# Dilated attention by token classes, an earlier turn of the fourth tile, and a projection started beside a rotation

## The chip, the cores and the metric

One of the eight cores of a Trainium2 chip runs the kernel; the metric is the time of one execution on the device in microseconds (us). The engines are TensorE (PE, with its weight loads as PEld), VectorE (DVE), ScalarE (ACT), GpSimd (POOL) and SyncE (SP), which only issues DMAs here.

## What is computed

Two transformer blocks on 512 tokens of width 1024, one after the other, in 32-bit floats. The first block is an FFN, a hybrid mixer and a second FFN; the mixer adds a branch of latent attention over the 128 best keys of an indexer and a branch of dilated attention, each under a gate. The second block is a mixer of MLA and retention, whose two halves are joined and projected, and a layer of experts found by keys (PEER). The part of the reference that is rewritten is the dilated branch: three groups of four heads, each with a window and a dilation, and a softmax over the groups by their log sums.

```python
DIL_PAIRS = ((128, 1), (512, 4), (2048, 16))

def dilated_group(q, k, v, window, dilation):
    offs = jnp.arange(window // dilation + 1) * dilation
    ...
        idx = tq[:, None] - offs[None, :]
        valid = idx >= 0
    ...
        s = jnp.where(valid[None, :, None, :], s, -jnp.inf)
        lse = jax.nn.logsumexp(s, axis=-1)
        p = jnp.exp(s - lse[..., None])
    ...
    wts = jax.nn.softmax(jnp.stack(lses, axis=0), axis=0)
    o = jnp.sum(wts[..., None].astype(v.dtype) * jnp.stack(outs, axis=0), axis=0)
```

A token of the second group sees the earlier tokens of its own class modulo 4, one of the third group those of its own class modulo 16, which lie in the same class modulo 4.

## The kernel before

Tokens are handled in four tiles of 128 (`NT` is 4, `P` is 128). A large product of 32-bit numbers is three products of split halves (`mm3`, lines 126 to 128): `h_hi` and `h_lo` for the activations, `whi` and `wlo` for the weights. Weights come by SP's queue (`raw`) and are split by ACT and DVE (`split`). PSUM tiles come from three rings, `ps`, `sc` and `po`. The instructions of each engine run in the order of its queue; that order is that of the code, in which generators yield so that two stages take turns, smoothed by a scheduler that sees the whole program.

At a boundary between sublayers (`boundary`) each tile's last products are joined to the residual `x`, its mean square is taken, the tile is scaled into `xs`, transposed on PE (`turn`, L414) and split into `h_hi` and `h_lo`. The first two tiles are turned inside the boundary; the third and fourth are handed on as two calls, `late[0]` (which also scales the fourth tile) and `late[1]`. The next sublayer calls them between its first products: `ffn` in its first chunk, where three products of 1024 by 128 are done in two halves of 256 tokens; `nform_steps` (latents of the first mixer and of MLA) between token tiles t = 0 to 3; `peer_queries` between its four blocks.

Dilated attention (`dilated`) treats two pairs of heads per group, pair after pair. For a pair, three parts (q, k, v) of width 384 are projected for all tiles; q and k are rotated (`rope`, six DVE operations, L606 to L611, into `dr`) and transposed by head pair (L885) into `dqT` and `dkT`; v stays as `dv`. Twelve chains follow, three groups for each of four query tiles, in a pipeline of three stages: first the scores (L623), masks added by a product with the identity (L628, one for each 128 keys), maximum, exponential; second the transposes of the exponentials (L642); third the products with v (L648). All groups see all key blocks up to their own (the first group two at most), so masked scores are computed too. After the third group of a tile `dil_join` weighs the three outputs. Between the rounds stand steps of the gate products (six products of width 512 each), and `merge` lets the indexer of the other branch run beside it: scores L786, then sixteen rounds of maximum and replacement on DVE (L799, L800) for each of three tiles. `heads_attend` of the latent branch follows.

In the second block `mixer2` runs MLA to the end (`oa`), then the retention in two halves: `ret_queries(1)` projects q and k of the second half, and only when all its tiles are done does it rotate and transpose them one by one (`then`, L611 to L1242); `ret_mix(0)` stands between its products. Then `oa` is transposed into `mT`, and the first eight steps of the output projection (`project_start`, six products each) fill the gaps of `ret_mix(1)`. A last fact for reading: L139 and L137 are the copies out of PSUM (`evac`), which alternate between ACT and DVE.

## Time and profile before

| | |
|---|---|
| time of the runs, us | 2829.49 median of 3 (2829.47 to 2831.88) |
| profiled execution, its own time | 2831.28 us |
| its span, first to last instruction | 2829.3 us |
| mean granted clock of PE | 0.989 |
| PE busy | 2757.3 us, 97% |
| DVE busy | 2058.4 us, 73% |
| ACT busy | 1151.5 us, 41% |
| POOL busy | 368.9 us, 13% |

A matmul's end is modelled and the next one starts before it, so the price of one is read from start to start where it can be. In a wait, the engine named behind the arrow is the one whose result was waited for last. PEclk 1.00 is the 2.4 GHz level, 0.50 the 1.2 GHz level.

### The profile page before, as it was taken

How to read it: one execution, taken by the hardware profiler on the slowest of the kernel's cores; microseconds unless marked ns; L12 is line 12 of the kernel's file. 1: busy time of each engine (PE TensorE's matmuls, PEld its weight loads, DVE VectorE, ACT ScalarE, POOL GpSimd, SP SyncE). 2: the span in 40 equal slices, each digit the busy share in tenths (PEclk: the TensorE clock that was granted, in tenths of full speed). 3: DMA queues.
4: the chain of work that ended last, by engine and by line, in shares of the span. 5: the costliest groups of instructions: out<-in, count | busy, mean ns of one | idle time of the engine just before them, and what ended most of it. 6: DMA issues, size and time to landing. Idle time of an engine off the chain costs nothing. (4 is left out here: it accounts for less than half of the span.)

```text
span 2829.3 us, 38970 instructions
## 1 busy us (share of the span) xinstructions
PE 2757.3 (97%) x14629; PEld 2331.7 (82%) x14629; DVE 2058.4 (73%) x4396; ACT 1151.5 (41%) x1925; POOL 368.9 (13%) x367
## 2 busy tenths in 40 slices
PE   8999999999999999999998999999999999999998
PEld 5877787879788777887787888999988888989896
DVE  6895247895656787226756789999877778877887
ACT  4343244333535444225523433765633333333333
POOL 0000000000000000001001002111121115343451
PEclk9999999999999999999999999999999999999999
DMA  7664221212034564321121227888899999888894
GB/s 276 223 235 144 89 103 47 93 61 90 16 132 147 190 228 178 112 99 63 61 67 74 90 96 246 310 290 299 318 347 330 328 322 336 326 313 307 300 344 181
DMA packets 152524, 552.55 MB, mean 195 GB/s; under 512 B 12368, under 2 KB 61840, under 8 KB 112656
## 3 DMA queue, kind: packets, MB, share of 16 engines
q1 hardware_dynamic: 111040, 403.86, 39.3%
q0 software_dynamic: 38848, 140.56, 14.0%
q10 hardware_dynamic: 2448, 5.65, 0.5%
q8 instruction: 114, 1.87, 0.3%
q14 instruction: 74, 0.61, 0.1%
HBM read 505.56 MB, written 44.47 MB: 194 GB/s over the span
## 5 line engine op out<-in xcount | busy, mean ns | idle before, releaser
L120 ACT ACTIVATE whi<-raw 128x1024 fp32r<-128x1024 f32 (+2 forms) x489 | 508.0, 1040 | 799.0 <-PE ps L127 381.6
L121 DVE TENSOR_TENSOR wlo<-raw,whi 128x1024 fp32r<-128x1024 f32 (+2 forms) x489 | 585.9, 1199 | 299.7 <-ACT whi L120 296.1
L126 PE MATMUL ps<-h_hi,whi 128*128 128x384 f32 (+2 forms) x1912 | 693.6, 363 | 10.8 <-ACT h_hi L131 6.4
L128 PE MATMUL ps<-h_hi,wlo 128*128 128x384 f32 (+2 forms) x1912 | 685.4, 359 | 3.1 <-DVE wlo L121 3.1
L127 PE MATMUL ps<-h_lo,whi 128*128 128x384 f32 (+2 forms) x1912 | 687.0, 359 | 0.7 <-DVE h_lo L132 0.7
L126 PEld LDWEIGHTS ps<-h_hi,whi 128*128 128x128 f32 x1912 | 362.1, 190 | 47.3 <-ACT h_hi L131 6.9
L128 PEld LDWEIGHTS ps<-h_hi,wlo 128*128 128x128 f32 x1912 | 361.9, 189 | 34.9 <-DVE wlo L121 4.0
L127 PEld LDWEIGHTS ps<-h_lo,whi 128*128 128x128 f32 x1912 | 362.6, 190 | 31.4 <-DVE h_lo L132 1.1
L126 PE MATMUL acc<-whi,wh 128*128 128x512 f32 x768 | 303.7, 396 | 2.4 <-ACT wh L131 2.4
L128 PE MATMUL acc<-whi,wl 128*128 128x512 f32 x768 | 303.9, 396 | 0.2 <-DVE wl L132 0.2
L127 PE MATMUL acc<-wlo,wh 128*128 128x512 f32 x768 | 303.7, 396 | 0.0
L1552 POOL DMA_INDIRECT erow<-in_eu,ids x128 | 142.5, 1113 | 651.1 <-DVE junk L1556 477.7
L131 ACT ACTIVATE wh<-wv 128x384 fp32r<-128x384 f32 x128 | 67.1, 524 | 339.7 <-issue 165.9
L1552 POOL DMA_INDIRECT erow<-in_ev,ids x128 | 166.7, 1302 | 225.6 <-DVE eacc L1564 194.1
L128 PEld LDWEIGHTS acc<-whi,wl 128*128 128x128 f32 x768 | 144.4, 188 | 35.9 <-DVE wl L132 0.8
L126 PEld LDWEIGHTS acc<-whi,wh 128*128 128x128 f32 x768 | 144.3, 188 | 35.9 <-ACT wh L131 2.7
L127 PEld LDWEIGHTS acc<-wlo,wh 128*128 128x128 f32 x768 | 144.4, 188 | 32.9
L1564 DVE SCALAR_TENSOR_TENSOR eacc<-erow,wgt,eacc 128x1024 f32<-128x1024 f32 x127 | 162.8, 1282 | 5.1 <-DMA erow<-in_ev,ids 3.5
L285 DVE SCALAR_TENSOR_TENSOR rows<-mraw,sil,rows 128x256 f32<-128x256 f32 x336 | 160.3, 482 | 6.6
L132 DVE TENSOR_TENSOR wl<-wv,wh 128x384 fp32r<-128x384 f32 x128 | 71.3, 557 | 122.5 <-ACT wh L131 114.8
L1556 DVE SCALAR_TENSOR_TENSOR junk<-erow,xr 128x1024 bf16<-128x1024 f32 x128 | 155.4, 1219 | 4.9 <-DMA erow<-in_eu,ids 4.9
L126 PE MATMUL ps<-whi,h_hi 128*128 128x384 f32 (+3 forms) x400 | 145.9, 366 | 7.1 <-ACT h_hi L131 6.5
(507 smaller groups left out, 4377.5 us busy)
## 6 DMA issues: line engine op xcount, KB each, us to landing
raw<-in_euT SPq DMA_DIRECT2D x64, 1024.0 KB
raw<-in_evp SPq DMA_DIRECT2D x64, 1024.0 KB
raw<-in_gu SPq DMA_DIRECT2D x44, 1024.0 KB
mraw<-in_wmod SPq DMA_DIRECT2D x24, 1024.0 KB
mraw<-in_wada SPq DMA_DIRECT2D x24, 1024.0 KB
dg<-gb SPq DMA_DIRECT2D x24, 1024.0 KB
gt<-dg SPq DMA_DIRECT2D x16, 1536.0 KB
raw<-in_dn SPq DMA_DIRECT2D x22, 1024.0 KB
```

The lines of the kernel that those rows point to most:

```text
L120: self.nc.scalar.activation(hi, r, AF.Copy)
L121: self.last_low = self.nc.vector.tensor_tensor(lo, r, hi.bitcast(F32), op=OP.subtract)
L126: mm(out, l[0], r[0], start=start, stop=False)
L127: mm(out, l[0], r[1], start=False, stop=False)
L128: self.last_mm = mm(out, l[1], r[0], start=False, stop=stop)
L131: self.nc.scalar.activation(hi, v, AF.Copy)
L132: self.last_pair = self.nc.vector.tensor_tensor(lo, v, hi.bitcast(F32), op=OP.subtract)
L285: nc.vector.scalar_tensor_tensor(rows, rv[:, k, :], c, rows, op0=OP.mult, op1=OP.add)
L1552: nc.gpsimd.indirect_dma_start(out=row, out_offset=None, in_=src, in_offset=bass.IndirectOffsetOnAxis(ap=ids[:, m:m + 1], axis=0))
L1556: nc.vector.scalar_tensor_tensor(junk, row, 1.0, xr, op0=OP.mult, op1=OP.mult, accum_out=act[:, m:m + 1])
L1564: nc.vector.scalar_tensor_tensor(eacc, row, wg[:, m:m + 1], eacc, op0=OP.mult, op1=OP.add)
```

## The change

Four things are edited. (1) Dilated attention: the first group keeps its chains over tiles of consecutive tokens, four per pair; the second and third group are computed together by classes modulo 4, four chains per pair: 128 queries against the 128 keys of their own class, one causal mask and one causal mask of every fourth, side by side in 256 columns. To this end q and k of these two groups are written into `dqT` and `dkT` in class order; v is projected first, written to DRAM (`dvs`) and read back twice, in token order (`dv`) and in class order (`cv`); the first group's outputs, maxima and sums go to DRAM (`dgs`) and come back in class order (`g0`), read after round `NT + 1` of the pipeline, for `dil_join`, which now runs per class; the transposed result `bT` is written back in token order. All of these DMAs are on POOL's queue, 11 per pair. The masks come first in their accumulation, and are a product of 256 columns. (2) The fourth tile is turned one block of products earlier in the FFN, the two latents and PEER's queries. (3) In `mixer2` the transposes of `oa` and four of the eight steps of `project_start` move into `ret_queries(1)`, the steps between its rotations; `mT` becomes two tiles, one for each half of the inner dimension. (4) Weights are packed in the order v, q, k.

```diff
-    m = [causal, k >= q, causal & ((q - k) % 4 == 0), (q - k) % 4 == 0,
-         causal & ((q - k) % 16 == 0), (q - k) % 16 == 0]
+    m = [k >= q, causal, causal & ((q - k) % 4 == 0)]
...
-                            if not j:
-                                late_h[n]()
+                            if not n and j in (0, 2):
+                                late_h[j // 2]()
...
-                    if late and t in (0, 3):
-                        late[t // 3]()
+                    if late and t in (0, 2):
+                        late[t // 2]()
...
             then(t, out[t][:, :width])
+            yield
...
+        self.dvs = [dg.tile([S, 384], F32, name=f"dvs{n}") for n in range(2)]
+        self.dgs = [dg.tile([S, 132], F32, name=f"dgs{n}") for n in range(2)]
...
-            dv = dil.tile([P, NT, 384], F32, name="dv")
+            dv = dil.tile([P, NT, P], F32, name="dv")
+            cv = dil.tile([P, NT, 256], F32, name="cv")
+            g0 = dil.tile([P, NT, 132], F32, name="dg0")
...
-                    if part == 2:
-                        self.evac(dv[:, t, :], out[t][:, :384])
+                    if part == 0:
+                        vt = self.misc.tile([P, 384], F32, name="dvt", tag="v")
+                        self.evac(vt, out[t][:, :384])
+                        nc.gpsimd.dma_start(self.dvs[pr][ts], vt)
...
-                    self.evac(dT[part][:, :, ts], p[:, :384].rearrange("p (g e) -> p g e", e=P))
+                    z = dT[part - 1]
+                    self.evac(z[:, 0, ts], p[:, :P])
+                    self.evac(z[:, 1:].rearrange("p g (j c) -> p g j c", j=NT)[:, :, :, 32 * t:32 * t + 32],
+                              p[:, P:384].rearrange("p (g m j) -> p g j m", g=2, j=NT))
+                if part == 0:
+                    nc.gpsimd.dma_start(dv, self.dvs[pr][:, :P].rearrange("(t p) e -> p t e", p=P))
+                    nc.gpsimd.dma_start(cv, self.dvs[pr][:, P:].rearrange("(c j) e -> c j e", j=NT))
...
+            mk = self.masks.rearrange("p a k -> p (a k)")
             for i in range(NT):
-                st = {}
-                for g in range(3):
-                    b0 = max(0, i - 1) if g == 0 else 0
-                    nb = i + 1 - b0
-                    masks = [(b * P, m[:, 2 * g + (0 if b == nb - 1 else 1), :]) for b in range(nb)]
-                    segs = []
-                    for s in range(2):
-                        rows = slice(64 * s, 64 * s + 64)
-                        segs.append((dT[0][rows, g, i * P:(i + 1) * P], dT[1][rows, g, b0 * P:(i + 1) * P], masks,
-                                     [dv[:, b0 + b, g * P + s * 64:g * P + s * 64 + 64] for b in range(nb)]))
-                    chains.append(self.dil_chain(work, st, segs, g, ob[:, i, pr * P:(pr + 1) * P]))
+                b0 = max(0, i - 1)
+                qs, ks = slice(i * P, (i + 1) * P), slice(b0 * P, (i + 1) * P)
+                heads = [([(dT[0][r, 0, qs], dT[1][r, 0, ks])],
+                          [[dv[:, b, 64 * s:64 * s + 64] for b in range(b0, i + 1)]])
+                         for s, r in enumerate((slice(0, 64), slice(64, P)))]
+                chains.append(self.dil_chain(work, heads, mk[:, (b0 - i + 1) * P:2 * P], self.dgs[pr][qs], None, None))
+            for j in range(NT):
+                js = slice(j * P, (j + 1) * P)
+                heads = [([(dT[0][r, g, js], dT[1][r, g, js]) for g in (1, 2)],
+                          [[cv[:, j, (g - 1) * P + 64 * s:(g - 1) * P + 64 * s + 64]] for g in (1, 2)])
+                         for s, r in enumerate((slice(0, 64), slice(64, P)))]
+                chains.append(self.dil_chain(work, heads, mk[:, P:], None, g0[:, j], ob[:, j, pr * P:(pr + 1) * P]))
...
+                if n == NT + 1:
+                    nc.gpsimd.dma_start(g0, self.dgs[pr].rearrange("(c j) e -> c j e", j=NT))
...
+    def dil_chain(self, work, heads, mask, dram, g0, out):
+        nc = self.nc
+        nb, w = len(heads[0][0]), mask.shape[-1]
+        st = {}
         def first():
-            if g == 0:
-                st["po"] = self.ps("po")
+            p = [self.ps(), self.ps()]
+            for s in range(2):
+                nc.tensor.matmul(p[s][:, :w], self.idb, mask, start=True, stop=False)
+            for b in range(nb):
+                for s in range(2):
+                    q, k = heads[s][0][b]
+                    nc.tensor.matmul(p[s][:, b * P:b * P + k.shape[-1]], q, k, start=False, stop=b == nb - 1)
+            if dram is not None:
+                st["z"] = work.tile([P, 132], F32, name="dz", tag="dz", bufs=4)
+                st["neg"], st["sums"] = st["z"][:, 128:130], st["z"][:, 130:132]
+            else:
                 st["neg"] = self.small.tile([P, 8], F32, name="neg", tag="neg")
                 st["sums"] = self.small.tile([P, 8], F32, name="sums", tag="sums")
-            for s, seg in enumerate(segs):
-                n = 2 * g + s
-                fs.append(self.attend(work, seg, 0.125, st["po"][:, n * 64:(n + 1) * 64], st["neg"], st["sums"], n))
-            for i in range(2):
-                for f in fs:
-                    f[i]()
+            lead = 0 if nb == 1 else 2
+            st["pr"] = []
+            for s in range(2):
+                mx = self.small.tile([P, 2], F32, name="mx", tag="mx")
+                nc.vector.tensor_reduce(mx[:, :nb], p[s][:, :w].rearrange("p (b k) -> p b k", b=nb), axis=AX.X, op=OP.max)
+                ng = st["neg"][:, lead:lead + 2 * nb].rearrange("p (b s) -> p s b", s=2)[:, s]
+                nc.vector.tensor_scalar(ng, mx[:, :nb], -0.125, None, op0=OP.mult)
+                pr = work.tile([P, 256], F32, name="pr", tag="pr", bufs=4)
+                for b in range(nb):
+                    n = lead + 2 * b + s
+                    bs = slice(b * (w // nb), (b + 1) * (w // nb))
+                    nc.scalar.activation(pr[:, bs], p[s][:, bs], AF.Exp, bias=st["neg"][:, n:n + 1], scale=0.125,
+                                         accum_out=st["sums"][:, n:n + 1])
+                st["pr"].append(pr)
         def second():
-            for f in fs:
-                f[2]()
+            st["pT"] = []
+            for pr in st["pr"]:
+                pt = self.ps("sc")
+                for b in range(w // P):
+                    nc.tensor.transpose(pt[:, b * P:(b + 1) * P], pr[:, b * P:(b + 1) * P], self.idf)
+                pT = work.tile([P, 256], F32, name="pT", tag="pT", bufs=4)
+                self.evac(pT[:, :w], pt[:, :w])
+                st["pT"].append(pT)
         def third():
-            for f in fs:
-                f[3]()
-            if g == 2:
-                self.dil_join(work, st["po"], st["neg"], st["sums"], out)
+            po = self.ps("po")
+            for s in range(2):
+                n = 0
+                for b, vals in enumerate(heads[s][1]):
+                    o = po[:, (2 * b + s) * 64:(2 * b + s + 1) * 64]
+                    for i, v in enumerate(vals):
+                        nc.tensor.matmul(o, st["pT"][s][:, n * P:(n + 1) * P], v, start=i == 0, stop=i == len(vals) - 1)
+                        n += 1
+            if dram is not None:
+                self.evac(st["z"][:, :P], po[:, :P])
+                nc.gpsimd.dma_start(dram, st["z"])
+            else:
+                self.dil_join(work, po, g0, st["neg"], st["sums"], out)
...
+        nc.gpsimd.tensor_copy(neg[:, :2], g0[:, 128:130])
+        nc.gpsimd.tensor_copy(sums[:, :2], g0[:, 130:132])
...
-                    self.transposed(ob[:, t, :], 2, t, bT[0], bT[1])
+                    self.transposed(ob[:, t, :], 2, 0, *(z.rearrange("p k (c j) -> p k j c", j=NT)[:, :, t] for z in bT))
...
+                pool = self.pool(st, "turneda", side="right", reuse_waits="tile")
+                aT = [pool.tile([P, 4, S], F32R, name=n) for n in ("aTh", "aTl")]
+                mT = [[z] for z in aT]
                 mix = self.ret_mix(0, t0, oy)
+                y = [[] for _ in range(NT)]
+                start = self.project_start(a["wo2"], mT, y)
                 for n, _ in enumerate(self.ret_queries(1, t1, h)):
-                    if n % 2:
-                        next(mix, None)
+                    if n < 16:
+                        if n % 2:
+                            next(mix, None)
+                        if n % 4 == 3:
+                            self.transposed(oa[:, n // 4, :], 4, n // 4, *aT, tag="sc")
+                    else:
+                        next(start)
                 for _ in mix:
                     pass
             pool = self.pool(st, "turned2", side="right", reuse_waits="tile")
-            mT = [pool.tile([P, KD, S], F32R, name=n) for n in ("mTh", "mTl")]
+            rT = [pool.tile([P, 4, S], F32R, name=n) for n in ("rTh", "rTl")]
...
-            if n % 2 == 0:
-                late[n // 2]()
+            if n < 2:
+                late[n]()
...
-        for part in range(3):
+        for part in (2, 0, 1):
```

On PE, beside the first pair's chains: a round before takes the fourth tile's second group (`dv` are its values, `pr` its exponentials, `dkT`, `dqT` the scores; `idb` is the identity that adds masks).

```order
L648 MATMUL po<-dv,pT 128x64 x6
L642 MATMUL sc<-idf,pr 128x128 x4
L623 MATMUL ps<-dkT,dqT 128x512 x2
L628 LDWEIGHTS idb
L628 MATMUL ps<-masks,idb 128x128
```

A round after, with a class chain (`cv` are values in class order):

```order
L984 MATMUL po<-cv,pT 128x64 x4
L972 MATMUL sc<-idf,pr 128x128 x4
L941 LDWEIGHTS idb
L941 MATMUL ps<-masks,idb 128x256
L941 LDWEIGHTS idb
L941 MATMUL ps<-masks,idb 128x256
L945 MATMUL ps<-dkT,dqT 128x128 x4
```

A chain's scores of width 512 with a mask product for each 128 keys have become scores of width 128, two groups by two heads, with one mask product per head; the six products with values that stood ahead of them have become four.

On PE, in the second block's mixer, around the transposes of the rotated retention queries (`rr`), before (`rat` and `rst` belong to the retention's outputs, `rkz` to its state):

```order
L1281 MATMUL po<-v_11183,rat 128x64 x2
L1242 MATMUL sc<-idf,rr 128x128 x8
L1313 MATMUL po<-v_11185,rkz 128x128 x4
L1242 MATMUL sc<-idf,rr 128x128 x8
L414 MATMUL sc<-idf,oa_12006 128x128 x4
L1313 MATMUL po<-v_11185,rkz 128x128 x2
L126 MATMUL ps<-whi,mTh 128x512
L414 MATMUL sc<-idf,oa_12006 128x128 x4
L127 MATMUL ps<-wlo,mTh 128x512
```

After, around the second such transposes (`aTh`, `aTl` are halves of the transposed `oa`):

```order
L127 MATMUL ps<-whi,aTl 128x512
L125 MATMUL ps<-whi,aTh 128x512
L1314 MATMUL sc<-idf,rr 128x128 x4
L126 MATMUL ps<-wlo,aTh 128x512
L127 MATMUL ps<-whi,aTl 128x512
L1385 MATMUL po<-v_10987,rkz 128x128 x4
L125 MATMUL ps<-whi,aTh 128x512
L126 MATMUL ps<-wlo,aTh 128x512
```

Where the transposes of two rotated tiles stood behind one another, products of the projection now stand ahead of each and behind it (ten between the first two tiles), and the transposes of `oa` stand earlier.

## Rows read from the trace of the kernel before

**Rows 1.** Windows: stretch, its us; busy of PE, PEld, DVE, ACT, POOL; PEclk; DMA.

```profile
549.10:635.80 86.70, 85.80 (x465) 60.70 (x465) 74.76 (x215) 37.17 (x95) 0.00 (x0) 0.96 0.21 70
689.00:729.20 40.20, 39.87 (x256) 27.59 (x253) 27.82 (x99) 18.97 (x65) 0.00 (x0) 1.00 0.20 70
```

**Rows 2.** Waits of PE: total us, times, longest.

```profile
PE ps L126 <- ACT h_hi L131: 12.9, 4, 3.6
...
PE sc L1242 <- DVE rr L611: 4.3, 2, 2.6
...
PE po L1313 <- DVE oy L1304: 2.2, 1, 2.2
```

**Rows 3.** Windows with the granted clock (PEclk, third number from the end).

```profile
437.44:440.85 3.41, 3.41 (x9) 2.64 (x10) 0.84 (x2) 1.06 (x1) 0.00 (x0) 0.50 0.00 0
597.87:604.70 6.83, 6.83 (x20) 3.72 (x20) 3.79 (x10) 1.55 (x4) 0.00 (x0) 0.50 0.47 154
1311.26:1314.67 3.41, 3.02 (x8) 2.65 (x9) 2.06 (x12) 1.30 (x3) 0.00 (x0) 0.50 0.00 0
1495.58:1505.82 10.24, 6.27 (x26) 5.43 (x27) 8.03 (x25) 2.51 (x6) 0.00 (x0) 0.50 0.01 2
1577.50:1584.33 6.83, 6.14 (x28) 5.85 (x29) 3.47 (x5) 1.40 (x3) 0.24 (x1) 0.50 0.09 34
```

**Rows 4.** Timeline of PE, second pair's chains: start, us busy.

```profile
719.19 0.71 PE L642 MATMUL sc<-idf,pr 128*128 128x128 f32 x5
...
721.00 1.55 PE L648 MATMUL po<-dv,pT 128*128 128x64 f32 x12
722.39 0.39 PE L642 MATMUL sc<-idf,pr 128*128 128x128 f32 x2
...
724.04 0.61 PE L628 MATMUL ps<-masks,idb 128*128 128x128 bf16 x8
```

**Rows 5.** Groups by line and shape, 540 to 740 us: busy us, mean ns.

```profile
L623 PE MATMUL ps<-dkT,dqT 64*128 64x256 f32 x40 | 10.5, 428 | 0.0
...
L623 PE MATMUL ps<-dkT,dqT 64*128 64x384 f32 x16 | 7.8, 632 | 0.0
...
L623 PE MATMUL ps<-dkT,dqT 64*128 64x512 f32 x16 | 6.7, 641 | 0.0
...
L623 PE MATMUL ps<-dkT,dqT 64*128 64x128 f32 x24 | 3.9, 322 | 0.0
```

**Rows 6.** Groups of DVE by shape, 496 to 640 us.

```profile
L800 DVE MATCH_REPLACE8 isc<-m,isc 128x512 f32<-128x512 f32 x16 | 10.8, 676 | 0.0
...
L606 DVE TENSOR_TENSOR rt<-ps,cos 128x192 f32<-128x192 f32 x8 | 2.8, 350 | 0.1
```

**Rows 7.** Timeline of PE, gate products in the first pair's chains.

```profile
563.01 0.39 PE L126 MATMUL ps<-h_hi,whi 128*128 128x512 f32 x1
...
565.09 0.55 PE L648 MATMUL po<-dv,pT 128*128 128x64 f32 x4
```

**Rows 8.** Timeline of POOL's queue; then tile sgl: ns min/median/max, first and last start.

```profile
267.96 0.71 POOL L323 DMA_DIRECT2D drow<-rowt  x1 [249.10 <-ACT rowt L321]
270.03 0.59 POOL L329 DMA_DIRECT2D grow<-drow  x1 [1.36 <-DMA drow<-rowt]
...
L1014 ACTq DMA_DIRECT2D sgl<-sg x4: 326/332/455, 779.6 to 844.4; - x4
L1015 ACT ACTIVATE sgl<-sgl x4: 1060/1061/1062, 782.8 to 850.0; 128x1024 f32<-128x1024 f32 x4
```

**Rows 9.** Timelines of PE, ACT and PE around the second FFN's start.

```profile
912.02 0.36 PE L126 MATMUL ps<-h_hi,whi 128*128 128x256 f32 x1
...
918.72 0.72 ACT L448 ACTIVATE xs<-x,rstd 128x512 f32<-128x512 f32 x1 [0.38 <-POOL rstd L148]
...
920.84 0.93 PE L414 MATMUL ps<-idf,xs 128*128 128x128 f32 x7
925.38 0.45 PE L126 MATMUL ps<-h_hi,whi 128*128 128x256 f32 x1 [3.62 <-ACT h_hi L131]
```

More of the change, by code (lines that the diff above doesn't have):

```diff
@@ L46 @@
 _at = 0
-for _n, _w in (("inv32", 32), ("inv16", 16), ("masks", 6 * 128), ("dmask", 8 * 128), ("xi", 4 * 128),
+for _n, _w in (("inv32", 32), ("inv16", 16), ("masks", 3 * 128), ("dmask", 8 * 128), ("xi", 4 * 128),
                ("zeta", 8), ("dec", 4)):
@@ L215, in tables @@
         lo, hi = CST["masks"]
-        mk = self.misc.tile([P, 768], F32, name="mk", tag="xn", bufs=1)
+        mk = self.misc.tile([P, 384], F32, name="mk", tag="xn", bufs=1)
         nc.scalar.dma_start(mk, a["cst"][:, lo:hi])
-        self.masks = f.tile([P, 6, P], BF, name="masks")
-        nc.vector.tensor_copy(self.masks, mk.rearrange("p (a k) -> p a k", a=6))
+        self.masks = f.tile([P, 3, P], BF, name="masks")
+        nc.vector.tensor_copy(self.masks, mk.rearrange("p (a k) -> p a k", a=3))
         self.causal = f.tile([P, P], F32, name="causal")
-        nc.vector.tensor_copy(self.causal, mk[:, :P])
+        nc.vector.tensor_copy(self.causal, mk[:, P:2 * P])
         self.rope_tables(f)
@@ L718, in mixer1 @@
                 for n, _ in enumerate(self.heads_attend(work, qT, kT, vv, oa,
-                                                        lambda i: [(0, mk[i])] if i else [(0, self.masks[:, 0, :])])):
+                                                        lambda i: [(0, mk[i])] if i else [(0, self.masks[:, 1, :])])):
                     next(more, None)
@@ L857, in dilated @@
         nc, a = self.nc, self.a
-        m = self.masks
         for pr in range(2):
             dT = [dil.tile([P, 3, S], F32, name=n) for n in ("dqT", "dkT")]
-            dv = dil.tile([P, NT, 384], F32, name="dv")
+            dv = dil.tile([P, NT, P], F32, name="dv")
+            cv = dil.tile([P, NT, 256], F32, name="cv")
+            g0 = dil.tile([P, NT, 132], F32, name="dg0")
             for part in range(3):
@@ L907, in dilated @@
                 whole = next(more, True)
-    def dil_chain(self, work, st, segs, g, out):
-        fs = []
+    def dil_chain(self, work, heads, mask, dram, g0, out):
+        nc = self.nc
+        nb, w = len(heads[0][0]), mask.shape[-1]
+        st = {}
         def first():
-            if g == 0:
-                st["po"] = self.ps("po")
+            p = [self.ps(), self.ps()]
[9 more added lines that the diff above has]
+            else:
@@ L935, in dil_chain, with dil_join @@
         return first, second, third
-    def dil_join(self, work, po, neg, sums, out):
+    def dil_join(self, work, po, g0, neg, sums, out):
         nc = self.nc
         v3 = lambda z: z.rearrange("p (g s) -> p s g", s=2)
+        nc.gpsimd.tensor_copy(neg[:, :2], g0[:, 128:130])
+        nc.gpsimd.tensor_copy(sums[:, :2], g0[:, 130:132])
         mn = self.small.tile([P, 2], F32, name="mn", tag="mn")
@@ L952, in dil_join @@
         tmp = work.tile([P, 6, 64], F32, name="dj", tag="dj", bufs=1)
-        nc.vector.tensor_tensor(tmp, po[:, :384].rearrange("p (n e) -> p n e", e=64),
-                                w[:, :6, None].to_broadcast([P, 6, 64]), op=OP.mult)
+        nc.vector.tensor_tensor(tmp[:, :2], g0[:, :P].rearrange("p (n e) -> p n e", e=64),
+                                w[:, :2, None].to_broadcast([P, 2, 64]), op=OP.mult)
+        nc.vector.tensor_tensor(tmp[:, 2:], po[:, :256].rearrange("p (n e) -> p n e", e=64),
+                                w[:, 2:6, None].to_broadcast([P, 4, 64]), op=OP.mult)
         tv = tmp.rearrange("p n e -> p (n e)")
@@ L1055, in project_start @@
             for t in range(NT):
-                self.project_part(z, y[t], t, 0, i, w)
+                if not y[t]:
+                    y[t].append(self.ps())
+                self.project_part(z, y[t][0], t, 0, i, w)
                 yield
@@ L1063, in project_part @@
             cs = slice(j * 512, (j + 1) * 512)
-            self.mm3(o, (z[0][:, k, ts], z[1][:, k, ts]), (w[0][:, cs], w[1][:, cs]), k == 0, k == KD - 1)
+            self.mm3(o, [q[u // 2][:, k % 4, ts] for q in z], (w[0][:, cs], w[1][:, cs]), k == 0, k == KD - 1)
     def project(self, ap, z, pool, join, scale, bias, y, rest=None, tags=("ps",) * NT):
@@ L1122, in mixer2 @@
             pool = self.pool(st, "turned2", side="right", reuse_waits="tile")
-            mT = [pool.tile([P, KD, S], F32R, name=n) for n in ("mTh", "mTl")]
+            rT = [pool.tile([P, 4, S], F32R, name=n) for n in ("rTh", "rTl")]
+            for z, r in zip(mT, rT):
+                z.append(r)
             def turn(t):
-                self.transposed(oy[:, t, :], 4, t, *mT, self.col("g_ret_norm_2"), None, 4, tag="po")
-            for t in range(NT):
-                self.transposed(oa[:, t, :], 4, t, *mT, tag="sc")
-            y = [[self.ps()] for _ in range(NT)]
-            start = self.project_start(a["wo2"], mT, [z[0] for z in y])
+                self.transposed(oy[:, t, :], 4, t, *rT, self.col("g_ret_norm_2"), tag="po")
             for n, _ in enumerate(self.ret_mix(1, t1, oy)):
@@ L1190, in mla @@
         work = self.pool(st, "work2", bufs=4, reuse_waits="tile")
-        for _ in self.heads_attend(work, qT, kT, vv, oa, lambda i: [(i * P, self.masks[:, 0, :])]):
+        for _ in self.heads_attend(work, qT, kT, vv, oa, lambda i: [(i * P, self.masks[:, 1, :])]):
             pass
@@ L1704, in build @@
             y = [[self.ps(), self.ps()] for _ in range(NT)]
-            for _ in self.project_start(a["wo"], z, [q[0] for q in y]):
+            z = [(q[:, :4], q[:, 4:]) for q in z]
+            for _ in self.project_start(a["wo"], z, y):
                 pass
```

## The prediction

> **What bounds the kernel now.** I read the busy time of each engine first, then windows over the stages that the change touches, then the waits of TensorE (PE), then the stretches at half clock. PE is the engine that is almost never idle. In the stage of the first dilated pair it is busy 85.80 of 86.70 us, although VectorE (DVE) has 74.76 us to do there; in the first 40.2 us of the second pair's chains it is busy 39.87 [rows 1]. So a microsecond of PE work taken out of these stages is worth nearly a microsecond, until another engine or a chain of latencies becomes the limit, and the rest can only come from two places: PE's few long waits and the half clock behind them. The waits are four for the first half of a turned tile (12.9 us in all, up to 3.6), three for a retention rotation (4.3), one for a retention output (2.2) [rows 2]. Behind four of these places the granted clock is 0.50, the 1.2 GHz level, for 3.41 to 10.24 us, and the busy time in such a stretch would need half as long at the full level [rows 3].
>
> **Dilated attention: work removed from PE.** Counts are instructions of the two programs, for both pairs together; prices come from the trace.
> Values: 108 products become 60 (28 on token order, 32 on classes). Each leaves two records; twelve records take 1.39 us (721.00 to 722.39) [rows 4], so 0.116 each: 96 fewer, -11.1 us.
> Transposes of the exponentials: 108 become 60, at no more than 0.71/5 = 0.14 us [rows 4]; the next group starts earlier than this one's end, so I take 0.115: -5.5 us (-6.8 at most).
> Scores: before 12, 20, 8 and 8 products of width 128, 256, 384, 512, with 3.9 + 10.5 + 7.8 + 6.7 = 28.9 us busy [rows 5]. After it is 36 of width 128 and 12 of width 256; at the groups' own means (3.9/12 and 10.5/20 us) 18.0. That gives -10.9; busy pieces overlap their neighbours by some 15 per cent, so -9 us.
> Masks: 104 fewer of width 128, 28 more of width 256. Eight narrow ones take 0.61 us busy [rows 4], 0.076 each, which includes the overlap; I take 0.065. A wide one stands nowhere in these chains: it costs between one narrow and two. Between, 1.5 narrow: -6.8 + 2.7, about -4 us (-2.6 to -6).
> Together -30 us of PE work (bounds -26 and -35).
>
> **Dilated attention: what is added.** The parts now come as v, q, k. Before, v's products stood behind the rotation of k; now the rotation of k is last. A rotation is six DVE operations of 0.35 us [rows 6], 2.1 us a tile; the first three tiles turn while products of the next tile run, and only the first two chains wait for early tiles, so about one tile per pair is uncovered: +4 us (0 if the gate products fill it, +8 if two tiles show).
> The pipeline has 10 rounds per pair for 14. The gate products that stand in its rounds (six of width 512 per step, 0.231 us each: nine between 563.01 and 565.09 [rows 7]) fall from 28 to 20 steps beside the first pair and rise from 4 to 12 beside the second; their sum does not change. But each round is shorter, and the chain score, maximum, exponential, transpose, value has the same latency: +4 us of waits (0 to 10).
> The first group's output goes to DRAM and back in class order. A write and a dependent read on POOL's queue: 2.07 us from the issue of the one to that of the other (267.96 to 270.03); a read of 512 KB from DRAM is used 3.2 us after its issue (779.6 to 782.8) [rows 8]. So some 5.5 us with POOL's small copies, against a round of about 6 us beside the first pair and 4 beside the second. It is late at most once per pair, at the first join, where DVE would hold the next reduces behind it; this is inside the +4. The writes of v and their two reads have the whole of two projections (each over 15 us) to land in: nothing.
> The Trainium skill ("DMA: Bandwidth & Descriptors", the anatomy of a DMA on the gpsimd path) gives about 2.0 us for each such DMA plus bytes over 436 GB/s, most of it the receipt of the write. An estimate from it for the write and the 264 KB read is 4.8 us, which speaks against a bounce in a stage this tight; the trace's 2.07 us agrees with its fixed part, and its sum would be the same.
> The 6.83 us at half clock lie inside this stage [rows 3], and cost 3.4 us now. Whether a drop comes in the new order can't be read; I credit half, -1.7 us.
> Dilated part: -30 + 4 + 4 - 1.7, about **-24 us** (-36 to -10).
>
> **The fourth tile's turn.** PE now meets the transposes of the fourth tile one block of products earlier, so that products stand between them and the first use of the result.
> Latents of the first mixer: 48 products of 0.231 us, 11 us, stand ahead of the turn and 24 (5.5 us) behind it. At the second FFN the row scaling of the fourth tile ends at 919.4, 7.4 us after the first product at 912.02, and the chain from the last transposes to the halves takes 4.5 us (920.84 to 925.38, the transposes in it) [rows 9]. If the first mixer's tile is no later than that, both are covered there. Of the 12.9 us for four waits [rows 2] the FFN's is 3.62 [rows 9], so the other three are 3.1 each on average: -3.1 and half of the 3.41 us busy at half clock, -4.8. At MLA's latents, a little narrower, the same: -3.1 and half of 3.02, -4.6 [rows 3].
> Second FFN: 72 products lie between 912.02 and 920.84, 0.1225 each [rows 9]. After 48 of them PE is at 917.9 and waits 1.5 us for the scaling; then 0.9 of transposes, 2.9 of products against a chain of 3.6: 0.7 more. So 2.2 in place of 3.62, -1.4, and I credit nothing for the clock.
> PEER's queries: the turn moves from behind 48 to behind 24 such products, 2.9 us earlier, so a similar 1.3 us of gain; of the 6.14 us busy at half clock [rows 3] I credit half of its cost, 1.5: -2.8.
> Sum **-14 us** (-10 to -18).
>
> **Projection beside the last rotation.** Between 1494 and 1506 PE waits 2.2 + 4.3 us [rows 2] and is busy 6.27 us at half clock, 3.1 us lost [rows 3]: 9.6 us in all. The change puts 24 products (5.5 us) between the four rotations. They are taken from the fillers of the retention mix that follows, itself a chain of waits; 39 products for 46 stand there, 1.6 us less to fill with. I expect that most of the waits and of the clock come back, some 8.6, less 1.6: **-7 us** (-3 to -11).
>
> **Sum.** -24 - 14 - 7 = -45 us. The profiled execution took 2831.28 us for a span of 2829.3; 2831.3 - 45 = 2786.3. The median of the runs, 2829.49, is 1.8 below the profiled one, so I forecast 2785. A difference under 0.2% (5.7 us) is what a measurement of this kernel can't tell from no change.
>
> **Rivals.**
> VectorE and latency set the dilated stage. For: DVE is busy 74.76 of 86.70 now. Of its work there, thirteen of the sixteen last maximum-and-replace pairs, some 2 x 0.676 us each [rows 6], slide out to the second pair's projection (-17.5), reduces fall (-5), rotations come in (+6): about 59 us, against PE's 85.8 - 1.7 - 15 - 8 x 1.39 = 58. Two engines that full, each waiting for the other, might need 70. Dilated part -10 in place of -24: 2799. Chance 0.22.
> All that is idle comes back: no rotation shows, the round trip and the shorter rounds are hidden, the clock stays whole (-35, -18, -11, 64 in all): 2766. Chance 0.10.
> The turns gain nothing: the scaling of the fourth tile is so late that PE waits in front of the transposes for as long as it did behind them. Rows 9 speak against it for the latents (919.4 against 11 us of products). 2797. Chance 0.08.
> Slower: the thin rounds let the clock fall. For it: the stage has the one drop today without a long wait ahead of it. About 96 us of PE work at full level are left in both pairs and their gates; were it all at the 1.2 GHz level it would take 96 us more, 2881. It ends slower than before from 45 us of that work at half level on. Against: one stretch of 6.83 us is all that the present rounds show, and gate products stand in all of the new ones. Chance 0.03. The Trainium skill ("TensorE: Matmul & The Clock Gate", Part 1) has the clock fall for an engine that idles; the trace agrees, 0.50 behind each of the long waits.
> No change that can be told, through several of these together: 0.03.
> My own case, 2774 to 2796, has 0.54. Range 2766 to 2808: the upper end is -10, -10 and -3. Faster 0.94, same 0.03, slower 0.03.
>
> **What would show it.** Right: PE's wait for the halves of a turned tile falls from 12.9 to about 4.5 us, with nothing at either latents; the wait for a rotation falls under 2 us, with a whole clock around the last retention queries; the first pair's chains last about 62 us, with PE still over 90 per cent busy; no long wait of DVE for the read of the first group. Wrong: DVE full and PE with many short waits there (first rival); new stretches at 0.50 in the second pair; a wait of DVE on POOL or on the DMA of several us at the first joins; waits in front of the transposes of the fourth tile.

## The result, and the profile after

The changed kernel takes 2791.72 us, median of 4 runs (2791.38 to 2793.91), against 2830.52: a ratio of 0.9866, 95% interval 0.985 to 0.9882, or 38.8 us less. The forecast was 2785 with a range of 2766 to 2808. The profiled execution has a span of 2789.5 us against 2829.3, 39.8 less; the account below is of these two. Of the executions below, one (a repeat of the kernel without the dependence on the first group) took 3817.83 us at a mean granted clock of 0.656 and is left out of every comparison.

I cut both traces at the same landmarks on PE (first instruction of a kind) and took differences of their starts, in us:

```text
stretch on PE                                         before     after   difference
first turned tile to the end of the first latents      48.26     42.73      -5.5
to the first dilated score                            105.07    108.44      +3.4
first pair's chains, second pair's projections        139.53    113.93     -25.6
second pair's chains                                   40.57     46.25      +5.7
latent attention                                       63.49     60.03      -3.5
combination and projection                            100.16    101.86      +1.7
second FFN, to the end of MLA's latents               424.86    417.04      -7.8
MLA                                                   136.46    139.45      +3.0
retention, projection, PEER's queries                 132.65    121.33     -11.3
before and behind these                              1638.26   1638.45      +0.2
```

PE's waits in the changed kernel (total, times, longest), those that answer to [rows 2] and those that are new:

```profile
PE po L897 <- DVE dr L612: 2.2, 1, 2.2
...
PE ps L125 <- DVE rt L610: 2.0, 3, 1.4
...
PE ps L414 <- ACT xs L448: 1.5, 1, 1.5
...
PE ps L126 <- DVE h_lo L131: 1.2, 2, 0.9
...
PE po L414 <- DVE xs L449: 0.9, 1, 0.9
PE ps L945 <- ACT dkT L136: 0.9, 1, 0.9
...
PE sc L1314 <- DVE aTl L421: 0.6, 1, 0.6
...
PE ps L125 <- ACT h_hi L130: 0.4, 1, 0.4
```

The four waits for the halves of a turned tile, 12.9 us, are now 0.4 and 1.2. What is left of them stands ahead of the transposes (`xs`, 1.5 and 0.9 us), where the fourth tile's scaling is waited for. The waits for a rotation of the retention's queries, 4.3 us, and the 2.2 us for a retention output are gone; 0.6 is waited for half of the transposed `oa`. New are 2.2 us for the rotation of q in the first pair, and 0.9 and 1.4 us around that of k in the second (the `rt` row holds two smaller ones as well; the `dkT` row is the first of k's two).

Windows of the changed kernel, columns as in [rows 1]: both pairs' chains, then all stretches at half clock between 500 and 1400 us, then the last retention rotations, and at the end the 20 us ahead of the stretch at 550.07.

```profile
545.90:607.00 61.10, 61.10 (x317) 42.23 (x315) 55.02 (x179) 30.13 (x93) 3.76 (x13) 0.97 0.24 83
659.50:707.20 47.70, 45.33 (x239) 34.16 (x238) 27.47 (x107) 18.28 (x72) 3.77 (x13) 0.86 0.23 75
526.18:529.59 3.41, 3.41 (x13) 3.40 (x12) 3.21 (x11) 0.28 (x1) 0.00 (x0) 0.50 0.40 153
550.07:553.48 3.41, 3.41 (x11) 2.73 (x10) 3.12 (x13) 1.54 (x6) 0.00 (x0) 0.50 0.00 0
662.71:676.36 13.65, 12.41 (x34) 7.96 (x34) 6.89 (x23) 2.77 (x12) 0.00 (x0) 0.50 0.18 61
1355.62:1362.44 6.82, 6.64 (x34) 6.28 (x34) 2.84 (x15) 3.51 (x19) 0.00 (x0) 0.50 0.01 2
1464.08:1476.00 11.92, 11.27 (x64) 8.99 (x62) 10.08 (x32) 3.72 (x11) 1.37 (x2) 1.00 0.00 0
529.60:550.07 20.47, 20.47 (x117) 17.88 (x116) 17.70 (x53) 7.00 (x12) 0.00 (x0) 1.00 0.25 78
```

The first pair's chains take 61.1 us with PE busy all of it and DVE 55.02: the forecast said about 62, with 58 and 59. The second pair's take 47.7, at a mean clock of 0.86, because 13.65 us of it run at the 1.2 GHz level although PE is busy 12.41 of them. Before, the two stages had one such stretch, of 6.83 us [rows 3]. The stretch at 550.07 has no wait ahead of it: PE's records fill the 20.47 us before it and all of its 3.41. The retention's rotations now run at the full clock, where 10.24 us were at half. In MLA a stretch of 6.83 us has appeared behind a wait (2.3 us, first scores) that stands in both kernels.

One round with a class chain in the first pair, on PE (start, busy):

```profile
582.23 1.00 PE L984 MATMUL po<-cv,pT 128*128 128x64 f32 x8
583.06 0.61 PE L972 MATMUL sc<-idf,pr 128*128 128x128 f32 x4
583.50 0.38 PE L941 MATMUL ps<-masks,idb 128*128 128x256 bf16 x2
583.82 0.71 PE L945 MATMUL ps<-dkT,dqT 64*128 64x128 f32 x8
584.46 0.50 PE L125 MATMUL ps<-h_hi,whi 128*128 128x512 f32 x1
```

Eight value records take 0.83 us from start to start, four transposes 0.44, two wide masks 0.32, four scores 0.64: 2.23 us in all. Summed in this way over the two stages, without waits and at half the price where the clock was 0.50, the kinds of work cost PE:

```text
start to start, both pairs, us    before    after    difference   forecast
values                             24.39    12.65       -11.74      -11.1
transposes of the exponentials     14.68     6.68        -8.00       -5.5
scores                             24.93    13.85       -11.08       -9
masks                               6.24     5.07        -1.17       -4
```

(Of the 108 transposes before, 100 stand ahead of the latent attention; their 13.59 us are scaled to 108.) That is -32 for a forecast of -30. The sum fits partly by luck: transposes and scores fell by 4.6 us more than forecast, masks by 2.8 less.

Part of this is a price that the forecast did not have, that of the step to a score. Two wide masks of the second pair, the first ahead of a transpose, the second ahead of a score:

```profile
696.22 0.27 PE L941 MATMUL ps<-masks,idb 128*128 128x256 bf16 x1
696.33 0.27 PE L972 MATMUL sc<-idf,pr 128*128 128x128 f32 x1
696.43 0.27 PE L941 MATMUL ps<-masks,idb 128*128 128x256 bf16 x1
696.64 0.49 PE L945 MATMUL ps<-dkT,dqT 64*128 64x128 f32 x2
```

The first takes 0.11 us to the next start, the second 0.21. By the medians of both stages at full clock a wide mask takes 0.109 us ahead of another and 0.203 ahead of a score; a narrow one before 0.056 and 0.149; a transpose before 0.110 and 0.203. So a wide mask costs as much as two narrow ones (the forecast took one and a half), and what stands right ahead of a score takes some 0.09 more. Where neither a wait nor half clock disturbs the reading, 21 transposes, 8 values and 2 masks stood there before, and 14 masks, 6 transposes and 1 value after: with the masks first in their accumulation, that price moved from one row to the other. Why the step costs this is not shown.

### The profile page after: what moved, and what is told of

It is laid out like the page before. It is cut to its first block, busy times and chain, and to the rows that moved or that the text cites. A ratio compares the mean times of both kernels' runs of the same rounds, so it can differ in the third digit from the quotient of the medians.

```text
span 2789.5 us, 38583 instructions
## 1 busy us (share of the span) xinstructions
PE 2726.3 (98%) x14409; PEld 2306.6 (83%) x14409; DVE 2049.3 (73%) x4376; ACT 1142.5 (41%) x1929; POOL 387.6 (14%) x405
```

## The experiments

**The three parts alone.** Each is the kernel before with one part of the change: the dilated part, the turns (with `if late and t in (0, 2)` and its two fellows), the projection beside the rotations.

> The kernel before with the dilated part of the change alone (classes, masks, DRAM bounces, order v, q, k). My theory: its gain is about 18 us, since 30 us of PE work go but PE now waits for the rotation of k at the start of the second pair and then runs some 14 us at half clock; so 2811 to 2814. Rival: the half clock there and the missing gain come from something that only the other parts bring (other load times, other phases of the clock); then alone it gains the 24 us that I forecast, 2806 or less.

Measured 2813.28 against 2831.02 in the same session, ratio 0.9933 (0.9916 to 0.995): 17.7 us less. My theory's number holds. Its trace shows the same 13.65 us at half clock at the same chains and the same waits of 0.93 and 1.45 us, so neither comes from the other parts.

> The kernel before with the earlier turn of the fourth tile alone (FFN, both latents, PEER's queries). My theory: the four places add up to about 19 us, the two latents 5 each, the second FFN 2 to 3, the queries 6, because the half clock behind the waits goes as well; 2811. Rival: what I forecast, 14 us, and the rest of the difference comes from other parts; 2816. With a clock drop at the first MLA scores, as the whole change shows it, 3 us more.

Measured 2815.4, ratio 0.9946 (0.9928 to 0.9963): 15.6 us less, nearer to the rival. By the landmarks of its profile the latents give 5.5, the second FFN with MLA's latents 7.8, the queries 2.7. My 6 for the queries was read from two landmarks of which the third part moves one.

> The kernel before with the transposes of the latent output and half of the projection's start moved beside the last rotations alone. My theory: 5 to 6 us, the two waits of 2.6 and 1.7 us and the half clock of 10 us go, and a little comes back as waits in the retention mix that follows; 2824 to 2825. Rival: 8 us or more, if those later waits belong to the whole change and not to this part.

Measured 2822.74, ratio 0.9975 (0.9963 to 0.9988): 8.3 us less; the rival's number. From the rotations to PEER's first scores its profile is 8.2 us shorter. The sum of the three medians is 41.6, the whole change 38.8: they add up within what the intervals leave. In the dilated part's profile the landmarks from the end of the first latents to the end of the latent attention give -21.2, more than its median shows; the other stages add 4.4 in that profile.

**Values last.** The order q, k, v again; the first group's values are copied straight to `dv`, the others go to class order through DRAM.

```diff
-        for part in (2, 0, 1):
+        for part in range(3):
...
+                        self.evac(dv[:, t, :], out[t][:, :P])
+                        vt = self.misc.tile([P, 256], F32, name="dvt", tag="v")
+                        self.evac(vt, out[t][:, P:384])
...
+                if part == 2:
+                    nc.gpsimd.dma_start(cv, self.dvs[pr].rearrange("(c j) e -> c j e", j=NT))
```

> The changed kernel with the parts in the order q, k, v again: the first group's values are copied straight to their tile in token order, only those of the second and third group go through DRAM, and are needed six rounds later. My theory: the rotation of k is covered again, so the waits of 2.2 us at the first transposes and of 0.9 and 1.5 us at the start of the second pair's chains go, and with them the 13.65 us at half clock; 6 to 10 us faster than the change, 2782 to 2786. Rival: the thin rounds of the second pair make the clock fall by themselves, so a stretch of half clock stays in that stage and the gain is under 4 us; a second rival, that the class-ordered values come late, would show as a wait of the products with values in the fifth chain.

Measured 2786.26 (ratio 0.9845, 0.9828 to 0.9863), 5.5 us below the change and 3.6 below its second measurement further down; the intervals overlap. Part of what I expected is in the profile: the waits for q in the first pair and k in the second are gone, the second pair's chains take 37.75 us for 46.25, at the full clock, and the values are not late. But a wait of 1.78 us stands in the second pair's first rounds (a gate product that waits for VectorE's work on the first chains), and no half clock follows it. And the second pair's projections lost 6.6 us to something that none of the theories had. Timeline of DVE and PE there:

```profile
624.66 0.35 DVE L608 TENSOR_TENSOR rt<-ps,sin 128x192 f32<-128x192 f32 x1
624.93 0.69 DVE L802 MAX8 m<-isc 128x8 f32<-128x512 f32 x1
625.53 0.34 DVE L609 TENSOR_TENSOR rt<-ps,cos 128x192 f32<-128x192 f32 x1
...
625.85 0.68 DVE L803 MATCH_REPLACE8 isc<-m,isc 128x512 f32<-128x512 f32 x1
626.44 0.35 DVE L610 TENSOR_TENSOR rt<-ps,sin 128x192 f32<-128x192 f32 x1
...
626.94 0.66 PE L125 MATMUL ps<-whi,h_hi 128*128 128x384 f32 x1 [4.11 <-DVE rt L610]
```

The indexer's last maxima, which the shorter first stage no longer holds, alternate with the rotation of q, and PE waits 4.11 us for a PSUM tile. In the change, with v first, they end at 634.4 and the rotation of q begins at 639.1. 6.83 us at half clock begin within that wait.

**Gate steps the other way.** `GF = (2, 1)`.

> The changed kernel with the steps of the gate products dealt out the other way: in every second turn beside the first pair, in every turn beside the second (some 10 and 20 steps for 20 and 12). My theory: the half clock in the second pair's chains starts with the waits of 0.9 and 1.5 us for the rotation of k and for the PSUM tile that it holds, so a stretch of 7 us or more at half clock stays at that place although the rounds are thicker. Rival: thin rounds make the clock fall; then the second pair's chains run at the full clock (6 us less there) and the first pair's thinner rounds show a stretch at half clock that they do not show now.

One execution, 2797.71 us. Beside the 3.41 us that the change has at the start of the first pair's chains, two stretches at half clock:

```profile
558.89:572.54 13.65, 13.65 (x41) 8.60 (x40) 7.28 (x21) 3.18 (x10) 1.11 (x2) 0.50 0.20 69
664.71:671.53 6.82, 5.86 (x15) 4.55 (x16) 4.82 (x16) 1.19 (x5) 0.00 (x0) 0.50 0.00 0
```

Thinned, the first pair's chains show a second stretch, of 13.65 us, with PE busy all of it; thickened, the second pair's still has one behind its waits (0.93 and 1.45 us again), but of 6.83 us. Both theories seem half right, as if the mix of a round counted as well as the wait. One execution can't show that: right ahead of the 13.65 us stands a wait of 0.57 us for the indexer, and a wait of that length for it is followed by no half clock in the kernel before, with values last, and in the last kernel below.

**Cover for the rotation of k.**

```diff
+                    if pr and part == 2:
+                        next(more, None)
```

> The changed kernel with one gate step placed behind each rotated tile of k of the second pair. My theory: the gate's products cover the rotation, PE's waits there (2.4 us) shrink to under 1 us, and the 13.65 us at half clock in that stage go or are halved; 4 to 8 us faster than the change, 2784 to 2788. Rival: the gate's PSUM tile is one that a tile still to be rotated holds, so PE waits just as long and the half clock stays; 2790 to 2793.

Measured 2789.26 (ratio 0.9854, 0.9834 to 0.9874): at best 2.5 us, which the intervals don't tell from nothing. At the place itself my theory held: no wait over 0.3 us and no half clock at the start of the second pair's chains. But the gate steps were missing in that pair's last rounds, of which 3.41 us run at half clock. The latent attention behind them took 66.91 us instead of 60.03, with a wait for its first values and half clock behind it; on PE, and the window that follows:

```profile
705.25 0.69 PE L649 MATMUL po<-vv,pT 128*128 128x64 f32 x2 [1.45 <-DVE neg L632]
```

```profile
705.26:712.09 6.83, 6.83 (x28) 5.88 (x29) 3.59 (x15) 3.89 (x16) 0.00 (x0) 0.50 0.54 183
```

The loss was moved, not removed: from the first pair's chains to the end of the latent attention this kernel takes 219.95 us, the change 220.21.

**Mixed orders.** First pair q, k, v, second pair v, q, k with the cover.

```diff
+            for at, part in enumerate(((0, 1, 2), (2, 0, 1))[pr]):
...
+                    if pr and part == 1:
+                        next(more, None)
```

> The first pair's parts in the order q, k, v, the second's in the order v, q, k with a gate step behind each rotated tile of k; values of the first group straight to their tile, those of the other two through DRAM. My theory: the wait of 2.2 us at the first pair's rotation of q, the two stretches of 3.4 us at half clock and most of the second pair's loss go, without the wait of 4.1 us that the order q, k, v brings to the second pair, where maxima of the indexer still stand between the rotations; 8 to 12 us faster than the change, 2780 to 2784. Rival: it gives no more than the order q, k, v for both pairs; 2785 to 2787.

Measured 2781.82 (ratio 0.9821, 0.9803 to 0.9839), as my theory said: 9.9 us below the change, clear of the intervals, and 8.0 below its second measurement, where they just overlap. The wait for q and the stretch at the second pair's start are gone; one of 3.41 us is left in the first pair's chains, and the loss in the latent attention (67.40 us) is still there.

**No dependence on the first group.**

```diff
-                if n == NT + 1:
-                    nc.gpsimd.dma_start(g0, self.dgs[pr].rearrange("(c j) e -> c j e", j=NT))
...
+            nc.gpsimd.dma_start(g0, self.dvs[pr][:, 128:260].rearrange("(c j) e -> c j e", j=NT))
```

> The changed kernel, but the tile of the first group's outputs is read from another place in DRAM before the chains begin, so that no join depends on what the first group wrote (the first group is left out of the result). My theory: the round trip through DRAM, 5.4 us from the last write to the small copies, costs nothing, since VectorE shows no wait for it; within 1.5 us of the change in the stage of the chains. Rival: joins that come late delay the maxima behind them; then the two chain stages get 3 to 6 us shorter.

One execution took 2779.1 us, and the second pair's chains 39.9 us for 46.25, which looked like the rival. The window of these chains:

```profile
658.30:698.20 39.90, 37.53 (x232) 29.33 (x230) 27.10 (x106) 18.24 (x71) 3.02 (x10) 1.00 0.19 62
```

The granted clock is 1.00 throughout, although the waits of 0.93 and 1.45 us at its start are the same. That, and not the trip, could be the gain of this stage; so the same kernel ran again, several times.

> The kernel without the dependence of the joins on the first group's write, again and timed (the first group is left out of its result). Theory: the trip through DRAM costs nothing and the missing stretch at half clock in the earlier profile was that execution's; so the median of the runs lies within 3 us of the changed kernel's, 2788 to 2793, and the profile shows a stretch at half clock in the second pair's chains again. Rival: the trip does cost, by thinner rounds around the joins and the half clock that they bring; then 2779 to 2784 and no such stretch.

Measured 2788.47, inside the theory's forecast, and the stretch was back:

```profile
663.54:677.19 13.65, 12.40 (x34) 7.96 (x34) 6.89 (x23) 2.78 (x12) 0.00 (x0) 0.50 0.17 60
```

Against the kernel before in its own session this is 43.4 us less (ratio 0.9843, 0.983 to 0.9856), where the change has 38.8 and 40.3. The intervals overlap, so the times alone leave room for a few us; the trace of the change shows no cost of the trip (POOL's queue, first pair):

```profile
578.20 0.54 POOL L988 DMA_DIRECT2D dgs<-dz  x1 [4.20 <-DVE dz L138]
580.66 0.54 POOL L923 DMA_DIRECT2D dg<-dgs  x1 [1.92 <-DMA dgs<-dz]
583.65 0.18 POOL L998 COPY neg<-dg 128x2 f32<-128x2 f32 x1 [2.44 <-DMA dg<-dgs]
```

2.46 us from the last write's issue to the read's, 2.99 to the copies: 5.4 in all, 5.5 forecast. DVE shows no wait for it in either pair. The Trainium skill ("DMA: Bandwidth & Descriptors", the anatomy of a DMA on the gpsimd path) gives 4.8 for the two as an estimate; the trace is 0.6 above it.

**The change again, and the first pair's tail.** The last kernel is that of the mixed orders with the gate steps kept out of the first pair's last two rounds, which a projection follows anyway.

```diff
-                    if k % GF[pr] == 0:
+                    if k % GF[pr] == 0 and (pr or n < 2 * NT):
```

> The changed kernel once more, unaltered, for a second profile. Theory: the stretch of 13.65 us at half clock in the second pair's chains belongs to the order of the work (the whole change and the dilated part alone both show it, 13.65 us at the same chains), so it stands there again, and so does the total within 3 us of 2791.7. Rival: which wait is followed by half clock differs from execution to execution; then that stretch is shorter or absent, as where the first group's trip through DRAM was cut (the same waits of 0.9 and 1.5 us, no stretch).

Measured 2789.86, five runs from 2780.98 to 2799.31. In the profile the stretch is longer than in the first, with PE busy in all but 0.85 us of it, while the one at the start of the first pair's chains is absent (one of 3.41 us stands near their end). The waits of 0.93 and 1.45 us are the same:

```profile
661.49:681.97 20.48, 19.63 (x57) 13.59 (x58) 7.97 (x28) 4.23 (x17) 0.56 (x1) 0.50 0.17 55
```

> The kernel of the mixed orders with no gate steps in the last two rounds of the first pair, where only transposes and values are left and the next projection follows; four steps more are left for the second pair and stand in its last rounds and ahead of the latent attention. My theory: the wait of 1.45 us at that attention's first values and the 6.83 us at half clock behind it go, 3 to 5 us faster than the mixed orders, 2777 to 2779. Rival: the steps only move, the first pair's stage waits as much as the second gains; 2781 to 2783.

Measured 2777.87, ratio 0.981 (0.9796 to 0.9823): 52 us below before and 12 below the change in the same session, clear of the intervals, and the fastest median here. Against the mixed orders the gain of 4.0 us is within the intervals; that it is this wait and stretch, the trace says. The chains of both pairs in its profile:

```profile
549.20:611.20 62.00, 61.06 (x340) 45.81 (x339) 55.78 (x169) 29.47 (x88) 5.05 (x16) 1.00 0.28 98
654.70:698.50 43.80, 43.46 (x273) 34.45 (x271) 28.81 (x113) 21.39 (x80) 3.75 (x13) 1.00 0.29 96
```

Both at the full clock, PE busy 61.06 of 62.00 and 43.46 of 43.80; the latent attention is back at 60.04 us, without the wait of 1.45. This profile is of the slowest of its five executions (2784.55 us): 13.65 us at half clock stand behind the retention's rotations in it, where the change and the projection's part alone had none.

## Why the prediction was right, and where it was off

The direction and the range held; the forecast was 7 us low. Term by term:

**PE work removed**: -30 forecast, -32 measured, with errors in both directions: -2.5 in the transposes, -2.1 in the scores, -0.6 in the values, +2.8 in the masks, which cost two narrow ones each and stand where the step to a score is paid. **Waits added**: +8 forecast for rotation, round trip and shorter rounds. PE's waits over 0.15 us from the first pair's projections to the latent attention were 1.6 us before and are 5.3 after: +3.7. Of these 5.3, 4.6 are rotations (2.2 for q of the first pair, which I had not named, and 2.4 for k of the second). Another 0.7 is a copy of v, whose trip I had put at nothing: VectorE's copy in the second pair waits 0.76 us until an earlier copy has been written to DRAM. The round trip was hidden, as far as the trace and the experiment without it show.

**Half clock in this stage** is the step that failed. I credited 1.7 us, half of what one stretch of 6.83 us cost. Instead there are three, 20.5 us together, and busy time in them needs half as long at the full level: some 10 us lost for 3.4 before, so +6. That the waits came out 4 us lower than forecast made up for more than half of this error, which is luck.

What makes the clock fall there stays open. Waits seem to have a part in it: of the six profiles with the two waits of 0.93 and 1.45 us for the rotation of k, five have a stretch there (13.65 us three times, 20.48, and 6.83 with thicker rounds), and the four without these two waits (values last, cover, mixed orders, last kernel) have none there. But the sixth profile with the same two waits has none either, values last has none behind its wait of 1.78 us, and the stretch at 550.07 comes behind 20 us without a wait. That thin rounds do it, the mechanism of my slowest rival, was argued and is not shown. The Trainium skill ("TensorE: Matmul & The Clock Gate", Part 1) ties the low level to an engine that has been idle. The waits ahead of the long stretches agree with it; the stretch at 550.07 does not, with PE busy by its records in all of it and ahead of it, nor does 19.63 us busy of 20.48 look like idling. In the prediction, "behind each of the long waits" holds for the waits that it lists; a wait of 2.3 us at MLA's first scores, in the same trace, is followed by none.

Dilated part in all: -24 forecast, -20 measured by the landmarks; -32, +3.7 and +6 make -22, and 2 us are not accounted for.

**The rival of VectorE** did not come: DVE is busy 55.02 of 61.10 us, and PE has no wait there.

**Turns**: -14 forecast, -16 measured. At the second FFN the 1.5 us ahead of the transposes came as computed, the 0.7 us behind them as 0.3, and no half clock followed, for which I had credited nothing. **Projection**: -7 forecast, -8 alone. Of the signs that I had named for being wrong, two came: half clock in the second pair, and waits in front of the fourth tile's transposes (1.5 and 0.9 us). Two sums in the prediction are off by some 2 us: with no gain of the turns the time is 2799 and not 2797, and the upper end of the range adds up to 2806.5 and not 2808; neither touches the outcome.

**Not in the sum**: +3.0 in MLA, where 6.83 us at half clock now follow an unchanged wait of 2.3 us (in other kernels here the same wait was followed by none, 3.41 or 6.83, and the stage was 0.4 or less, 1.5 and 3.0 us longer than before); +1.7 in the combination, of which 0.5 is a longer wait for the transposed outputs (2.1 us for 1.56). With that same wait the combination took from 99.99 to 103.36 us in other kernels here, so the rest may be the execution's. -20 - 16 - 8 and +4.7 make -39, the span's 39.8.

## What to carry to other kernels

Where one engine is full, count its instructions and price them from start to start, then look for what the removed work had covered: here the rotation of the last projected part, and the fillers of later rounds. Fillers are a fixed stock; placing them where a wait is visible moves the wait to where they are missing, so take them first from places that dense work follows anyway. Where instructions change their order, price also the step from one kind to the next, not each kind by itself. Before reading a few microseconds as an effect, run the same kernel twice: stretches at half clock come and go between executions.

## What was not expected of the hardware

From start to start at 2.4 GHz a mask product by the identity takes 0.109 us for 256 columns and 0.056 for 128, but 0.203 and 0.149 right ahead of a score with 64 rows; a transpose takes 0.110, and 0.203 there. Ahead of the latent attention's scores, with 96 rows, a narrow mask takes 0.060. PE stayed at the 1.2 GHz level for 20.48 us in which its records show it busy for 19.63, and in another place fell to it behind 20.47 us of unbroken work. And the changed kernel's runs, under 0.1% apart at first (2791.38 to 2793.91), later spread from 2780.98 to 2799.31.
